# An up-projection by seven block products: four sums of weights instead of five, and shared sums built up in PSUM by TensorE

## Chip, cores and metric

One Trainium2 core runs the kernel. The metric is device time in microseconds, from the first to the last instruction of the program on that core, as the median of several executions. Lower is better. TensorE (PE) does matrix products into PSUM, VectorE (DVE) and ScalarE (ACT) read PSUM and SBUF, GpSimd (POOL) works on SBUF only, and SyncE (SP) issues DMAs.

## What is computed

One layer of an encoder on a sequence of 1024 frames of width 1024: a token-mixing half with two attention branches, a residual with layer norm, and then a gated MLP with a short causal convolution. The change concerns the first step of the MLP, the up-projection `h @ w_up`, and what it needs made ready.

```python
h = _layer_norm(x) * (1.0 + sc2) + sh2
u = _causal_depthwise_conv(h @ w_up[l], conv_w[l], conv_b[l])
a, val = jnp.split(u, 2, axis=-1)
y = (jax.nn.silu(a) * val) @ w_down[l]
x = _layer_norm(alpha * x + (1.0 + g2) * y, ln2_g[l], ln2_b[l])
```

`h` is 1024 x 1024, `w_up` is 1024 x 5632 (2816 columns for `a`, 2816 for `val`). All in float32.

## The kernel before

**Float32 by three products.** Every float32 operand is split into a high part (`F32R`, made by a cast, mostly on ACT) and a low part (operand minus high part, a subtraction on POOL or DVE). A product of two operands is then three matmuls: high x high, high x low, low x high. One matmul has a stationary block of 128x128 and a moving block of 128x512.

**Seven products in place of eight.** The up-projection runs over 22 column blocks `c` of 128 columns of `a` and the matching 128 columns of `val`. For one `c` the frames are cut into two halves of 512 and the inner dimension of 1024 into two halves of 512; the weights of `c` are four blocks `b11`, `b21` (for `a`, upper and lower half of the inner dimension) and `b12`, `b22` (for `val`), each 512 x 128 and held as 128x4x128. A direct calculation takes eight block products. `up` (L979) uses Strassen's scheme with seven, `m1` to `m7`. Each block product is `product` (L731): four slices of the inner dimension times three matmuls, 12 matmuls, all added up in a PSUM bank of its own (pool `mxp`, six banks). Stationary operands lie in ten slots (`slot`, L943) and are made by `operand` (L721): a sum of two weight blocks if one is wanted (L725), a cast to the high part on ACT (L727), a subtraction for the low part (L728). Moving operands are seven sums or blocks of `h`, held split for the whole stage: `h_11` and `h_11p12` belong to the first half of the frames alone, the other five (`h_11p22`, `h_21p22`, `h_21m11`, `h_22`, `h_12m22`) need the second half.

The results go to two SBUF tiles, `u[0]` for `a` and `u[1]` for `val`, 128x1026, one buffer each, whose halves are `ua0`, `ua1`, `uv0`, `uv1`. DVE and ACT add the seven products into them (L988 to L1005). `conv` (L957) then runs the convolution on one of the two: a scaled copy into a PSUM tile `pcv` of two banks, one buffer (ACT, L961), two multiply-adds (DVE, L963), for `a` also a Silu (ACT, L966) and the product with the other half's result (DVE, L967). The result `y` goes to DRAM (L975).

**Early products.** Two of the seven, `m3` (with `h_11`) and `m5` (with `h_11p12`), need only the first half of the frames. For the first `HEAD` = 8 blocks they are computed ahead by `head` (L750), copied by ACT to SBUF (L757) and stored to DRAM tile `md` (L758); `up` reads them back (L984, L985). `ready` (L743) loads the weights of a block and makes the two operands, `b12 - b22` (the sum on POOL) and `b22`. Blocks 0 to 2 (`EARLY` = 3) run beside the norms of the second half, blocks 3 to 7 beside `turned_1`. The stage `up` takes the blocks in the order 0, 8, 1, 9, ..., 7, 15, 16, ..., 21, so that blocks with five products left and blocks with seven alternate.

**What lies ahead of the up-projection.** For each half of the frames: `merge` (the two branches), `mix` (output projection, L795), `residual` (L829), `norms` (L843). `mix` scales the rows of `w_out` by a gate (L105), casts (L106) and subtracts (L107); in the second half's `mix` the last four of the eight weight blocks are prepared before use, their subtraction being on POOL, that of the first four on DVE. `turned_0` (L875) transposes the first half of `h`, stores it to DRAM (`hx`) and makes `h_11` and `h_11p12`; it runs beside the second half's `merge` and `mix`. `turned_1` (L883) transposes the second half, reads the first half back (`hf`), and makes the other five moving operands with `put` (L867: sum L870, cast L872, subtraction L873). `spread_row` (L185) makes a row of a gate for the down-projection out of small products (`gc` on DVE, L191; `psrow` on PE, L192).

**What sets the order.** Python calls give the program order, but the tile framework orders each engine's instructions when it builds the program: the instruction streams in the profile are interleaved differently from the source. On the chip every engine then takes its instructions in that fixed order, and waits on semaphores where an operand or a buffer isn't ready.

Of the kernel before, what the change touches and what calls it, by code (L numbers as in the profile page):

```python
# [42 lines left out]
def body(ctx, tc, a, out):  # L43
# [116 lines left out]
    def ada_late(v, half, pieces, accs, psum):  # L160
        """One half of a modulation vector, a block of its weights at a time."""
        acc = None
        ws = []
        for k in range(KD + 1):
            if k < KD:
                ws.append(pieces())
                sy.dma_start(out=ws[k], in_=ada_src(v, half * H, H)[:, k : k + 1, :])
            if k > 0:
                acc = acc or accs()
                ada_acc(acc, k - 1, ws[k - 1][:, 0, :])  # L170
            if k == KD:
                ada_fold(psum(), acc, v, half * H, H, v != 3)
            yield
# [56 lines left out]
    class Stream:  # L230
        """Projections run in order, each one's weights loaded and split ahead of it."""
# [289 lines left out]
    # the attention steps, head by head, and the projections that run between them  # L521
# [183 lines left out]
    h_11, h_11p12 = operands(hap, "ha"), operands(hap, "hb")  # L705
# [15 lines left out]
    def operand(slot, tmp, x, y=None, op=None, eng=ve, lo=po):  # L721
        w = slot([P, 2, 4, P], F32R)
        if y is not None:
            t = tmp.tile([P, 4, P], F32, name=nm("wt"), tag="ht", bufs=2 if tmp is mxb else 3)
            eng.tensor_tensor(out=t, in0=x, in1=y, op=op)  # L725
            x = t
        se.copy(out=w[:, 0], in_=x)  # L727
        lo.tensor_sub(out=w[:, 1], in0=x, in1=w[:, 0])  # L728
# [14 lines left out]
    def ready(c):  # L743
        if c < HEAD:
            b12, b22 = raw(c, 1, wp, "ws")
            raws.clear()
            lo = ve if c >= EARLY else po
            readied.append((operand(head_slot, mxb, b12, b22, ALU.subtract, po, lo), operand(head_slot, mxb, b22, lo=lo)))

    def head(c):  # L750
        w3, w5 = readied.pop(0)
        for i, ps in ((1, product(w3, h_11)), (0, product(w5, h_11p12))):
# [4 lines left out]
            se.copy(out=t, in_=ps)  # L757
            se.dma_start(out=md[c, i], in_=t)  # L758
        ready(c + 2)

    if True:
# [105 lines left out]
        def put(dst, x, y=None, op=None, e=(ve, ve, po), pool=mxb, n=2):  # L867
            if y is not None:
                t = pool.tile([P, H], F32, name=nm("ht"), tag="ht", bufs=n)
                e[0].tensor_tensor(out=t, in0=x, in1=y, op=op)  # L870
                x = t
            (e[1].copy if e[1] is se else e[1].tensor_copy)(out=dst[0], in_=x)  # L872
            e[2].tensor_sub(out=dst[1], in0=x, in1=dst[0])  # L873

        def turned_0(tiles):  # L875
            for j in range(4):
                x, y = turned(tiles, j), turned(tiles, j + 4)
                se.dma_start(out=hx[j], in_=x)
                se.dma_start(out=hx[j + 4], in_=y)
                put(h_11[j], x, e=(None, se, ve))  # L880
                put(h_11p12[j], x, y, ALU.add, (ve, ve, po))

        def turned_1(tiles):  # L883
            for j in range(4):
                h11, h12 = [th.tile([P, H], F32, name=nm("hf"), tag="hf", bufs=4) for _ in range(2)]
                sy.dma_start(out=h11, in_=hx[j])
                sy.dma_start(out=h12, in_=hx[j + 4])
# [35 lines left out]
    h_11p22, h_21p22, h_21m11, h_22, h_12m22 = [operands(hbp, f"hc{i}") for i in range(5)]  # L923
# [33 lines left out]
    def conv(c, b, gate=None):  # L957
        y = fu.tile([P, S], F32, name=nm("y"), tag=f"y{b}", bufs=2 - b)
# [3 lines left out]
        for d in (1, 2):  # L962
            ve.scalar_tensor_tensor(out=ps if d == 1 or b == 0 else y, in0=u[b][:, 2 - d : S + 2 - d],  # L963
                                    scalar=cp[:, 2 - d : 3 - d], in1=ps, op0=ALU.mult, op1=ALU.add)
        if b == 0:
            se.activation(out=ps, in_=ps, func=AF.Silu)  # L966
            ve.tensor_tensor(out=y, in0=ps, in1=gate, op=ALU.mult)  # L967
        return y
# [9 lines left out]

    def up(c):  # L979
        b12, b22 = raw(c, 1, hbp, "fs")  # L980
        b11, b21 = raw(c, 0, *((wp, "ws") if c not in order[:2] else (hbp, "fs")))
        stored()
        if c < HEAD:
            sy.dma_start(out=uv0, in_=md[c, 0])  # L984
            sy.dma_start(out=uv1, in_=md[c, 1])  # L985
        else:
            m3 = product(operand(slot, ff, b12, b22, ALU.subtract), h_11)
            se.copy(out=uv1, in_=m3)  # L988
            m5 = product(operand(slot, ff, b22), h_11p12)
            se.copy(out=uv0, in_=m5)  # L990
        m1 = product(operand(slot, ff, b11, b22, ALU.add), h_11p22)
        ve.tensor_sub(out=ua0, in0=m1, in1=uv0)
        ve.tensor_tensor(out=uv0, in0=uv0, in1=uv1, op=ALU.add)
        ve.tensor_tensor(out=uv1, in0=m1, in1=uv1, op=ALU.add)
        m2 = product(operand(slot, ff, b11), h_21p22)
        se.copy(out=ua1, in_=m2)
        ve.tensor_sub(out=uv1, in0=uv1, in1=m2)
        m6 = product(operand(slot, ff, b11, b12, ALU.add, po, ve), h_21m11)
        ve.tensor_tensor(out=uv1, in0=m6, in1=uv1, op=ALU.add)  # L999
        yv = conv(c, 1)  # L1000
        m4 = product(operand(slot, ff, b21, b11, ALU.subtract, po, ve), h_22)
        ve.tensor_tensor(out=ua1, in0=m4, in1=ua1, op=ALU.add)
        ve.tensor_tensor(out=ua0, in0=m4, in1=ua0, op=ALU.add)
        m7 = product(operand(slot, ff, b21, b22, ALU.add), h_12m22)
        ve.tensor_tensor(out=ua0, in0=m7, in1=ua0, op=ALU.add)  # L1005
        pending.append((c, conv(c, 0, yv)))
# [181 lines left out]
```

## Time and profile before

| | |
|---|---|
| Median of 3 runs | 1644.32 us (1643.68 to 1644.86) |
| Profiled execution, span | 1644.2 us |
| PE busy | 1565.3 us, 95% |
| DVE busy | 1147.5 us, 70% |
| ACT busy | 780.7 us, 47% |
| POOL busy | 561.3 us, 34% |
| mean granted TensorE clock | 0.980 |
| first matmul of `up` starts at | 1006.9 us |
| last matmul of `up` ends at | 1391.6 us |

Rows of groups give the line, engine, operation, output tile `<-` input tiles, then busy time. Rows of the timeline begin with start and duration in us; a bracket holds the idle time of the engine just before and what ended it. The windows table gives, for each stretch, its length, and then for PE, PEld (weight loads), DVE, ACT, POOL the busy us with the number of instructions, then the granted clock (1.00 is full), the share of DMA and GB/s. The duration of a matmul includes its way through the array, and successive ones overlap, so PE's rate is read from the count of a window.

### The profile page before, as it was taken

The page shows a single profiled execution, that of the slowest core. Times are in us where ns is not written, and L with a number is a line of the kernel's source. Part 1 is how long each engine was busy: PE and PEld are TensorE (multiplying, and loading weights), DVE is VectorE, ACT ScalarE, POOL GpSimd, SP SyncE. Part 2 cuts the span into 40 slices and gives each one's busy share as a digit, 9 for nine tenths or more (in the row PEclk, how much of TensorE's full clock was granted, in tenths as well). Part 3 has the DMA queues.
Part 4 walks back from the last instruction along what each step waited for, and adds up shares of the span by engine and source line. Part 5 has one row for each costly group of instructions (what it writes and reads, how often), then busy time and mean ns, then how long its engine had stood idle before and what let it go on. Part 6 is the DMA issues. An engine that isn't in the chain of part 4 may idle for free.

```text
span 1644.2 us, 22112 instructions
## 1 busy us (share of the span) xinstructions
PE 1565.3 (95%) x7821; PEld 1303.5 (79%) x7821; DVE 1147.5 (70%) x2293; ACT 780.7 (47%) x1382; POOL 561.3 (34%) x521
## 2 busy tenths in 40 slices
PE   6899999999999999998997978999999999999996
PEld 3788898889889888877876767888888888888885
DVE  6738776686677665536599786999998776544617
ACT  3547556655565555654235265544454444331311
POOL 1111213112322322222053756554455443650602
PEclk9999999999999999999998999999999999999998
DMA  9133432342252333246546245323322212761611
GB/s 346 45 97 115 140 91 77 113 129 65 72 173 84 103 96 123 71 160 222 170 154 230 95 168 160 115 106 126 127 100 94 77 71 90 261 207 39 204 40 52
DMA packets 81823, 205.81 MB, mean 125 GB/s; under 512 B 8560, under 2 KB 17328, under 8 KB 81712
## 3 DMA queue, kind: packets, MB, share of 16 engines
q1 hardware_dynamic: 77104, 197.49, 36.6%
q10 hardware_dynamic: 4608, 6.90, 1.1%
q8 instruction: 62, 1.02, 0.3%
q14 instruction: 49, 0.40, 0.1%
HBM read 157.14 MB, written 38.83 MB: 119 GB/s over the span
## 4 chain that ended last, share of the span: by engine, by line
PE 77%; DVE 13%; DMA 4%; ACT 2%; POOL 2%; issue 2%; SPq 0%; ACTq 0%; DVEq 0%; POOLq 0%
PE psu L211 8%; PE psu L209 8%; PE psu L210 8%; PE psd L1032 5%; PE psd L1031 5%; PE psd L1033 5%; PE pso L507 4%; PE psg L209 4%; PE psg L210 4%; PE psg L211 3%; PE pst L492 3%; PE psq L209 2%; PE psq L211 2%; PE psq L210 2%; PE psv L304 2%; PE psv L303 2%
## 5 line engine op out<-in xcount | busy, mean ns | idle before, releaser
L96 POOL TENSOR_TENSOR wl<-ws,wh 128x1024 fp32r<-128x1024 f32 x54 | 133.0, 2465 | 317.1 <-ACT wh L95 273.0
L1025 DVE TENSOR_TENSOR gl<-gs,gh 128x512 fp32r<-128x512 f32 x41 | 64.8, 1593 | 102.5 <-ACT gh L1024 97.7
L1031 PE MATMUL psd<-dd,gh 128*128 128x512 f32 x328 | 127.6, 389 | 0.0
L1032 PE MATMUL psd<-dd,gh 128*128 128x512 f32 x328 | 127.6, 389 | 0.0
L1033 PE MATMUL psd<-dd,gl 128*128 128x512 f32 x328 | 127.4, 389 | 0.0
L457 ACT ACTIVATE s<-s,mx 128x640 f32<-128x640 f32 (+7 forms) x128 | 94.6, 739 | 47.5 <-DVE mx L451 46.0
L496 ACT CAST pt<-pst 128x512 fp32r<-128x512 f32 (+1 forms) x192 | 82.4, 452 | 67.8 <-PE pst L492 63.1
L209 PE MATMUL psq<-h1h,wh 128*128 128x512 f32 x256 | 104.6, 410 | 0.0
L209 PE MATMUL psu<-hc,wx 128*128 128x512 f32 x264 | 104.4, 396 | 0.0
L210 PE MATMUL psu<-hc,wx 128*128 128x512 f32 x264 | 104.4, 396 | 0.0
L211 PE MATMUL psu<-hc,wx 128*128 128x512 f32 x264 | 104.4, 396 | 0.0
L209 PE MATMUL psg<-h1h,wh 128*128 128x512 f32 x256 | 103.8, 406 | 0.0
L210 PE MATMUL psq<-h1l,wh 128*128 128x512 f32 x256 | 101.1, 395 | 0.0
L211 PE MATMUL psq<-h1h,wl 128*128 128x512 f32 x256 | 100.9, 394 | 0.0
L497 DVE TENSOR_TENSOR pt<-pst,pt 128x512 fp32r<-128x512 f32 (+1 forms) x192 | 96.8, 518 | 5.9 <-ACT pt L496 4.0
L210 PE MATMUL psg<-h1l,wh 128*128 128x512 f32 x256 | 100.2, 392 | 0.0
L211 PE MATMUL psg<-h1h,wl 128*128 128x512 f32 x256 | 100.2, 391 | 0.0
L507 PE MATMUL pso<-pt,vs 128*128 128x256 f32 x608 | 92.2, 290 | 3.1 <-DVE o L512 1.7
L963 DVE SCALAR_TENSOR_TENSOR pcv<-u,convp,pcv 128x1024 f32<-128x1024 f32 x66 | 84.9, 1287 | 13.5 <-ACT pcv L961 12.6
L961 ACT ACTIVATE pcv<-u,convp 128x1024 f32<-128x1024 f32 x44 | 53.2, 1210 | 86.3 <-DVE u L999 34.6
L1019 POOL TENSOR_TENSOR dd<-ws,dd 128x1024 fp32r<-128x1024 f32 x25 | 63.3, 2542 | 88.2 <-ACT dd L1018 88.1
L507 PEld LDWEIGHTS pso<-pt,vs 128*128 128x128 f32 x608 | 81.8, 191 | 12.5 <-ACT pt L496 4.0
(281 smaller groups left out, 4539.8 us busy)
## 6 DMA issues: line engine op xcount, KB each, us to landing
ws<-in_w_up SPq DMA_DIRECT2D x52, 512.0 KB, 3.8
wa<-in_w_ada SPq DMA_DIRECT2D x64, 256.0 KB, 3.0
ws<-in_w_down SPq DMA_DIRECT2D x28, 512.0 KB, 3.4
yd<-y SPq DMA_DIRECT2D x22, 512.0 KB, 2.6
gs<-yd SPq DMA_DIRECT2D x44, 256.0 KB, 3.6
wa<-in_w_ada SPq DMA_DIRECT2D x8, 1024.0 KB, 12.0
ws<-in_w_qk SPq DMA_DIRECT2D x16, 512.0 KB, 4.8
ws<-in_w_g SPq DMA_DIRECT2D x16, 512.0 KB, 3.7
```

The source lines that it names most:

```text
L96: po.tensor_sub(out=lo, in0=st, in1=hi)
L209: pe.matmul(ps, wh, xh, start=start, stop=False)
L210: pe.matmul(ps, wh, xl, start=False, stop=False)
L211: pe.matmul(ps, wl, xh, start=False, stop=stop)
L457: se.activation(out=st[:, 0:nk], in_=st[:, 0:nk], func=AF.Exp, scale=-1.0, bias=prev, accum_out=sm)
L496: se.copy(out=dh, in_=src)
L497: ve.tensor_sub(out=dl, in0=src, in1=dh)
L507: pe.matmul(ps[:, 0:256], vs[:, j0 + j, :], pt[c][j // 4][:, j % 4, :], start=j == 0 and c == 0, stop=j == nj - 1 and c == 1)
L963: ve.scalar_tensor_tensor(out=ps if d == 1 or b == 0 else y, in0=u[b][:, 2 - d : S + 2 - d], scalar=cp[:, 2 - d : 3 - d], in1=ps, op0=ALU. ...
L1031: pe.matmul(ps[n], g[0][:, ts], d[0][:, halves(n)], start=start, stop=False)
L1032: pe.matmul(ps[n], g[0][:, ts], d[1][:, halves(n)], start=False, stop=False)
L1033: pe.matmul(ps[n], g[1][:, ts], d[0][:, halves(n)], start=False, stop=stop)
```

## The change

The seven products are arranged in another scheme (of Winograd's kind). The weights of a block are named `w11`, `w21` (for `a`), `w12`, `w22` (for `val`). Sums of weights: `s1 = w21 + w22`, `s2 = s1 - w11`, `w12 - s2`, `w11 - w21`: four, all on DVE, where there were three on DVE and two on POOL (before, in a block with early products, two and two). All low parts are made on POOL; before, two of a block's were on DVE. Moving operands: `h_11`, `h_21` from the first half; `h_22`, `h_t1 = h21' - h11`, `h_t2 = h22 - h_t1`, `h_t3 = h22 - h21'`, `h_t4 = h21 - h_t2` (`h21'` being the transposed block `x` of the second half). In `turned_0` a sum on DVE falls away; in `turned_1` there are, as before, three sums on DVE, one on POOL, three low parts on DVE, two on POOL, but `h_22` comes first.

Sums that several results share are no longer formed by DVE out of separate products: one PSUM bank, `main`, takes four products one after the other, and another, `side`, two. After each product ACT or DVE reads the bank's state, and the next product adds on to it. A block with all seven products had, after its products, eight DVE additions and three ACT copies; now it has three and four. A block with early products had eight and one; now it has five and none.

The early products are now `w11 h_11` and `w12 h_21`; ACT copies the first, DVE adds the first to the second, and both are stored. The sum on POOL in `ready` falls away. `conv` is now called for `a` first, then for `val`, both after the block's last product; before, `val` came first, ahead of the last two products. The buffers change with it (`y` two, `p1` one, `ht` four).

```diff
-    def product(w, h):
-        ps = mxp.tile([P, H], F32, name=nm("psu"), tag="mm")
+    def product(w, h, ps=None):
+        on = ps is not None
+        if not on:
+            ps = mxp.tile([P, H], F32, name=nm("psu"), tag="mm")
         for k in range(4):
-            mm3(ps, w[:, 0, k, :], w[:, 1, k, :], h[k][0], h[k][1], k == 0, k == 3)
+            for a_, b_ in ((0, 0), (0, 1), (1, 0)):
+                first = k == 0 and (a_, b_) == (0, 0) and not on
+                pe.matmul(ps, w[:, a_, k, :], h[k][b_], start=first, stop=k == 3 and a_ == 1, skip_group_check=on)
         return ps
...
-            b12, b22 = raw(c, 1, wp, "ws")
+            w11, w12 = raw(c, 0, wp, "ws")
...
-            readied.append((operand(head_slot, mxb, b12, b22, ALU.subtract, po, lo), operand(head_slot, mxb, b22, lo=lo)))
+            readied.append((operand(head_slot, mxb, w11, lo=lo), operand(head_slot, mxb, w12, lo=lo)))
...
-            se.copy(out=t, in_=ps)
+            if i == 0:
+                se.copy(out=t, in_=ps)
+                p1 = t
+            else:
+                ve.tensor_tensor(out=t, in0=ps, in1=p1, op=ALU.add)
             se.dma_start(out=md[c, i], in_=t)
...
-                put(h_11p12[j], x, y, ALU.add, (ve, ve, po))
+                put(h_21[j], y, e=(None, ve, po))
...
-                put(h_11p22[j], h11, y, ALU.add, (ve, se, po), th, 6)
-                put(h_21p22[j], x, y, ALU.add, (ve, se, po), th, 6)
-                put(h_21m11[j], x, h11, ALU.subtract, (ve, se, ve), th, 6)
                 put(h_22[j], y, e=(None, se, ve))
-                put(h_12m22[j], h12, y, ALU.subtract, (po, se, ve), th, 6)
+                t1 = put(h_t1[j], x, h11, ALU.subtract, (ve, se, po), th, 6)
+                t2 = put(h_t2[j], y, t1, ALU.subtract, (ve, se, po), th, 6)
+                put(h_t3[j], y, x, ALU.subtract, (po, se, ve), th, 6)
+                put(h_t4[j], h21, t2, ALU.subtract, (ve, se, ve), th, 6)
...
     def up(c):
+        w21, w22 = raw(c, 1, hbp, "fs")
+        w11, w12 = raw(c, 0, *((wp, "ws") if c not in order[:2] else (hbp, "fs")))
         stored()
+        early = c < HEAD
+        if early:
+            p1 = fu.tile([P, H], F32, name=nm("p1"), tag="p1", bufs=1)
+            sy.dma_start(out=p1, in_=md[c, 0])
+            sy.dma_start(out=ua0, in_=md[c, 1])
         else:
+            main = product(operand(slot, ff, w11), h_11)
+            se.copy(out=ua0, in_=main)
+        s1 = ff.tile([P, 4, P], F32, name=nm("s1"), tag="ht", bufs=4)
+        ve.tensor_tensor(out=s1, in0=w21, in1=w22, op=ALU.add)
+        s2 = ff.tile([P, 4, P], F32, name=nm("s2"), tag="ht", bufs=4)
+        ve.tensor_tensor(out=s2, in0=s1, in1=w11, op=ALU.subtract)
+        if early:
+            main = product(operand(slot, ff, s2), h_t2)
+            add(ua1, main, p1)
+            side = product(operand(slot, ff, s1), h_t1)
+            add(uv1, side, p1)
+        else:
+            side = product(operand(slot, ff, s1), h_t1)
+            se.copy(out=uv1, in_=side)
+            product(operand(slot, ff, s2), h_t2, main)
+            se.copy(out=ua1, in_=main)
+        def third():
+            product(operand(slot, ff, w12, s2, ALU.subtract), h_22, side)
+            add(ua1, side, ua1)
+        if not early:
+            third()
+        product(operand(slot, ff, w11, w21, ALU.subtract), h_t3, main)
+        add(uv1, main, uv1)
+        if early:
+            third()
+        else:
+            m2 = product(operand(slot, ff, w12), h_21)
+            add(ua0, m2, ua0)
+        product(operand(slot, ff, w22), h_t4, main)
+        if early:
+            add(uv0, main, p1)
+        else:
+            se.copy(out=uv0, in_=main)
+        y = fu.tile([P, S], F32, name=nm("y"), tag="y", bufs=2)
+        conv(c, 0, y)
+        conv(c, 1, y)
+        pending.append((c, y))
```

More of the change, by code (lines that the diff above doesn't have):

```diff
@@ L744, in ready @@
         if c < HEAD:
-            b12, b22 = raw(c, 1, wp, "ws")
+            w11, w12 = raw(c, 0, wp, "ws")
             raws.clear()
             lo = ve if c >= EARLY else po
-            readied.append((operand(head_slot, mxb, b12, b22, ALU.subtract, po, lo), operand(head_slot, mxb, b22, lo=lo)))
+            readied.append((operand(head_slot, mxb, w11, lo=lo), operand(head_slot, mxb, w12, lo=lo)))
     def head(c):
-        w3, w5 = readied.pop(0)
-        for i, ps in ((1, product(w3, h_11)), (0, product(w5, h_11p12))):
+        w11, w12 = readied.pop(0)
+        p1 = None
+        for i in range(2):
+            ps = product((w11, w12)[i], (h_11, h_21)[i])
             if c < EARLY:
@@ L922, in body @@
     hb_cm, hbp = opened(name="hb", bufs=1, side="right")
-    h_11p22, h_21p22, h_21m11, h_22, h_12m22 = [operands(hbp, f"hc{i}") for i in range(5)]
+    h_22, h_t1, h_t2, h_t3, h_t4 = [operands(hbp, f"hc{i}") for i in range(5)]
     th_cm, th = opened(name="th", bufs=2)
@@ L977, in body, with add @@
     raws.update({(0, 1): start[0], (0, 0): start[1]})
+    def add(out, x, y):
+        ve.tensor_tensor(out=out, in0=x, in1=y, op=ALU.add)
     def up(c):
-        b12, b22 = raw(c, 1, hbp, "fs")
-        b11, b21 = raw(c, 0, *((wp, "ws") if c not in order[:2] else (hbp, "fs")))
+        w21, w22 = raw(c, 1, hbp, "fs")
+        w11, w12 = raw(c, 0, *((wp, "ws") if c not in order[:2] else (hbp, "fs")))
         stored()
-        if c < HEAD:
-            sy.dma_start(out=uv0, in_=md[c, 0])
-            sy.dma_start(out=uv1, in_=md[c, 1])
-        else:
[L987 to L999, printed above, removed]
```

29 lines of the change are left out of this document (11 added, 18 removed).

## The prediction

> **What bounds the kernel now.** I read the page's engine shares first, then busy time by windows around the touched stages, then the timelines of the engines where PE isn't full.
>
> ```profile
> PE 1565.3 (95%) x7821; PEld 1303.5 (79%) x7821; DVE 1147.5 (70%) x2293; ACT 780.7 (47%) x1382; POOL 561.3 (34%) x521
> ```
> ```profile
> 900.00:950.00 50.00, 46.52 (x194) 37.11 (x193) 37.71 (x73) 18.16 (x26) 35.79 (x19) 0.97 0.27 95
> 950.00:1000.00 50.00, 36.71 (x162) 28.11 (x161) 38.08 (x60) 31.44 (x54) 27.94 (x21) 0.86 0.52 173
> 1150.00:1200.00 50.00, 50.00 (x217) 40.44 (x217) 47.20 (x55) 24.84 (x37) 24.88 (x19) 1.00 0.30 106
> 1350.00:1400.00 50.00, 50.00 (x218) 40.64 (x217) 33.92 (x37) 22.20 (x28) 18.43 (x12) 1.00 0.22 77
> ```
>
> In the up-projection (third and fourth row) PE never pauses and has the full clock: 217 matmuls in 50 us, 0.230 us each, so a product of 12 takes 2.76 us. DVE, at 47.2 of 50 us where short and long blocks alternate, is nearly full but holds nobody up. Ahead of it (second row) PE is idle for 13 of 50 us and partly at half clock. So DVE work taken out of the up-projection buys nothing by itself; the time can only move in the 100 us before it, or upwards, if PE begins to wait.
>
> **Part by part.**
>
> *Count of matmuls.* 84 per block before and after, 60 where two products are early, with the same three weight loads per slice. No change: 0.
>
> *turned_0 and ready, beside the second mix.* Here the change takes work away.
>
> ```profile
> 894.18 0.68 DVE L870 TENSOR_TENSOR ht<-h,h 128x512 f32<-128x512 f32 x1
> 895.84 1.79 DVE L870 TENSOR_TENSOR ht<-h,h 128x512 f32<-128x512 f32 x1
> 898.61 1.79 DVE L870 TENSOR_TENSOR ht<-h,h 128x512 f32<-128x512 f32 x1
> 902.35 4.52 DVE L107 TENSOR_TENSOR wl<-ws,wh 128x1024 fp32r<-128x1024 f32 x2
> ```
> ```profile
> 898.59 1.05 ACT L106 CAST wh<-ws 128x1024 fp32r<-128x1024 f32 x1
> ```
> ```profile
> 904.69 0.50 PE L807 MATMUL psm<-wl,mh 128*128 128x512 f32 x1 [3.35 <-DVE wl L107]
> ```
> ```profile
> 906.00:908.00 2.00, 2.00 (x6) 1.62 (x5) 0.92 (x2) 0.00 (x0) 2.00 (x1) 0.50 0.65 236
> 908.00:910.00 2.00, 2.00 (x7) 1.56 (x7) 2.00 (x1) 0.00 (x0) 2.00 (x2) 0.67 0.72 252
> 910.00:912.00 2.00, 2.00 (x11) 1.62 (x10) 1.70 (x2) 1.50 (x3) 2.00 (x1) 1.00 0.00 0
> ```
>
> PE waits 3.35 us for a low part of `w_out` that DVE gets to at 902.35, after three sums (0.68 + 1.79 + 1.79 = 4.3 us) that the change removes. Without them DVE could be there at 898.1; the cast it reads ends at 898.59 + 1.05 = 899.64, so the gain is 2.7 us. Behind the pause PE runs at half clock: 6 and 7 matmuls in two windows that would hold 11 each, as the third does: 9 matmuls of 2.00 / 11 = 0.18 us, 1.6 us. PE could be up to 3.35 + 1.6 = 5.0 us earlier. Next comes POOL:
>
> ```profile
> 899.93 1.62 POOL L725 TENSOR_TENSOR wt<-ws 128x512 f32<-128x512 f32 x1
> 903.64 2.15 POOL L725 TENSOR_TENSOR wt<-ws 128x512 f32<-128x512 f32 x1
> 918.25 2.43 POOL L107 TENSOR_TENSOR wl<-ws,wh 128x1024 fp32r<-128x1024 f32 x1
> ```
> ```profile
> 920.73 0.50 PE psm L807
> 921.50 0.69 DVE xr L839
> ```
>
> In the chain of waits POOL's last low part of `w_out` ends at 918.25 + 2.43 = 920.68, PE goes on at 920.73 and the residual begins at 921.50. The two sums in `ready`, 1.62 + 2.15 = 3.8 us, stood ahead of it on POOL and go. So the residual can start 3.8 us earlier, the lesser of POOL's 3.8 and PE's 5.0. Bounds: 0, if a DMA or the order keeps its place, to 5.0. I take 3.8, as both chains shorten by about that.
>
> *The early products' additions.*
>
> ```profile
> 944.53 0.57 ACT L757 COPY mc<-psu 128x512 f32<-128x512 f32 x1
> 949.90 0.59 ACT L757 COPY mc<-psu 128x512 f32<-128x512 f32 x1 [0.42 <-PE psu L211]
> 956.56 0.56 ACT L757 COPY mc<-psu 128x512 f32<-128x512 f32 x1
> ```
> ```profile
> 952.09 1.29 DVE L113 BATCH_NORM_STATS2 st<-xr 128x6 f32<-128x512 f32 x2 [2.29 <-POOL xr L849]
> 957.68 0.69 DVE L728 TENSOR_TENSOR wl<-ws,wl 128x512 fp32r<-128x512 f32 x1 [1.16 <-ACT wl L727]
> 967.44 1.75 DVE L873 TENSOR_TENSOR hc<-h,hc 128x512 fp32r<-128x512 f32 x1
> 962.93 1.21 DVE L870 TENSOR_TENSOR ht<-hf,h 128x512 f32<-128x512 f32 x1 [1.56 <-DMA hf<-hx]
> 989.45 1.35 DVE L191 TENSOR_SCALAR gc<-ones,modc 128x128 f32<-128x128 f32 x1
> 1167.29 0.68 DVE L992 TENSOR_TENSOR u<-psu,u 128x512 f32<-128x512 f32 x1
> ```
>
> Eight copies on ACT (above, the second one of each of the first three blocks) become additions on DVE, 0.7 us each by the nearest row, 1167.29. Two of these three copies lie in pauses of DVE (2.29 us before 952.09, 1.16 before 957.68), the first doesn't: 0.7 (0 to 2.1). Two more additions fall into `turned_1`, which DVE fills: 1.4 (0 to 1.4). The last three come when `turned_1` is through and DVE is slack: 0. The ACT queue issues the store behind each addition, so casts of `turned_1` stand queued behind that wait, and DVE's low parts wait for them; ACT, busy for 31.4 of the 50 us, has room, and without it the wait is again DVE's 0.7.
>
> *turned_1.* Same number of operations on each engine, so from 962.93 to about 991 it still takes DVE's 28 us. `h_22` now comes first and needs no read back: its low part (0.7 uncontended; 1.75 at 967.44 beside POOL) fits into the 1.56 us pause for `hf`: -0.7 (0 to -1.6).
>
> ```profile
> PE psrow L192 <- DVE gc L191: 12.5, 4, 5.0
> ```
>
> PE's pauses in that stretch, 12.5 us in four, wait for DVE and shift with it.
>
> *The up-projection.* Chain, full block: conv on `a` may start one product before the block ends.
>
> ```profile
> 1157.24 0.39 PE L211 MATMUL psu<-ha,wx 128*128 128x512 f32 x1
> ```
> ```profile
> 1160.75 1.21 ACT L961 ACTIVATE pcv<-u,convp 128x1024 f32<-128x1024 f32 x1 [2.60 <-DVE y L963]
> 1161.90 0.58 ACT L988 COPY u<-psu 128x512 f32<-128x512 f32 x1
> 1165.11 1.01 ACT L966 ACTIVATE pcv<-pcv 128x1024 f32<-128x1024 f32 x1 [1.11 <-DVE pcv L963]
> ```
> ```profile
> 1161.99 1.29 DVE L963 SCALAR_TENSOR_TENSOR pcv<-u,convp,pcv 128x1024 f32<-128x1024 f32 x1
> 1163.79 1.28 DVE L963 SCALAR_TENSOR_TENSOR pcv<-u,convp,pcv 128x1024 f32<-128x1024 f32 x1
> 1166.15 1.23 DVE L967 TENSOR_TENSOR y<-pcv,y 128x1024 f32<-128x1024 f32 x1 [0.23 <-ACT pcv L966]
> ```
>
> Let T be the end of the block's last product. `ua0` is added at T - 2.76 + 0.7 = T - 2.1; scaled copy 1.2, two multiply-adds 2.5: `ua` is free at T + 1.7. Silu 1.0, the copy for `val` 1.2, two multiply-adds 2.5: `uv` is free at T + 6.4. The next block's second product (`side`) ends at T + 5.5; its eviction into `uv1` runs from T + 6.4 to T + 7.1, and the third product, in `main`, ends at T + 8.3, when `side` is wanted again. The tightest margin is 1.2 us. DVE's load falls: per pair of blocks, 144 x 0.23 = 33 us, 16 additions become 8, four low parts go, three sums come, at 0.7 each -6.3 us. POOL's two sums a block become two low parts, and ten operand slots give lead. I take 0, the margin being positive and DVE slack; bounds 0 to +18 (second rival). A gain is excluded, since PE is never idle there.
>
> Here a rule can be weighed. In the trace every product has its own bank, so evictions may trail: the product that the copy at 1161.90 reads had its last matmul started at 1157.24, and ended one step later, 4.4 us before the copy. The Trainium skill, "PSUM — Partial Sum Buffer", section on bank collisions, says that a bank must be guarded by semaphore between TensorE's write and another engine's access, whatever the addresses. By that rule PE cannot add to `main` or `side` during an eviction: still 0 where the other bank's 2.76 us cover it, rival 2's sum where they don't. No row of this trace shows it, since no bank is reused half way.
>
> *After it.* The last block's `y` is ready last in both kernels, and the down-projection begins with other blocks: 0.
>
> **Sum**, against the profiled execution's 1644.2 us (0.1 under the median): -3.8 + 0.7 + 1.4 - 0.7 + 0 = -2.4, or 1641.8; with the 0.1, 1641.9.
>
> **Rivals.**
>
> 1. *The gain ahead is kept whole.* All additions find pauses and PE's 5.0 us come through, with 0.7 in `turned_1`: -5.7, 1638.6. For it: DVE has the pauses of 2.29, 1.16 and 1.56 us. Against: POOL's chain gave only 3.8, and DVE is full from 963 to 991.
>
> 2. *PE waits for evictions of `main` and `side`* (the slower side). Decisive is whether an eviction starts more than 2.76 - 0.6 = 2.2 us after its product. Today's lag of 4.4 is 2.2 too many. A full block has a free product (`w12 h_21`) to put between; a block with early products has none but the next block's. One such wait in each of the 8: 8 x 2.2 = 18 us; some of it filled by the next block's products, I take 13 and, with the -2.4, 1655. Against: DVE gets slack, and the trailing of 4.4 us harms nobody today, so nothing shows it to be a minimum.
>
> 3. *The clock falls in the up-projection.* The trace has half clock after a pause of 3.35 us (above); it shows none after short ones:
>
> ```profile
> 974.00:976.00 2.00, 1.20 (x5) 0.62 (x3) 2.00 (x2) 2.00 (x5) 2.00 (x2) 0.96 0.42 131
> 976.00:978.00 2.00, 1.55 (x9) 1.32 (x10) 2.00 (x3) 0.52 (x2) 1.65 (x2) 1.00 0.01 4
> ```
>
> If one product per block ran at half clock: 22 x 2.76 = 61 us, 1703. The Trainium skill, "TensorE: Matmul & The Clock Gate", section on PSUM-queue depth-cycling, says that cycling through PSUM banks can idle PE briefly so often that its clock drops again and again; that would make it so. The 0.8 us idle in the first of these rows, followed by 1.00, disagrees with it.
>
> 4. *Nothing moves:* the changed order eats up the 2.4: 1644.3.
>
> **How the numbers follow.** A measurement of this kernel can tell some 0.2%, 3.3 us, from no change: below 1641.0 is faster, above 1647.6 slower. Forecast 0.46: its terms put -2.4 near that line, with 0.17 beyond it (the 5.0, or the additions hidden) and 0.29 within. Rival 1 has 0.22, faster. Rival 2 0.25, rival 3 0.03, both slower. Rival 4 0.04. So faster 0.39, same 0.33, slower 0.28. The range reaches from 1636, 2.6 us under rival 1 (PE pauses for 13 us from 950 to 1000, of which more could go), to 1657, over rival 2's middle; outside are the rest of rival 2, rival 3 and a few points below, some 0.2. The forecast's own range is 1639 to 1645.
>
> **What would show it.** Right: 217 matmuls in each 50 us of the up-projection at clock 1.00, DVE there under 42 of 50 us; the pause of 3.35 us before the second `mix`'s third weight block gone or under 1 us; the residual's first row near 917.7; the first product of `up` 2 to 3 us earlier. Wrong in the up-projection: idle time of PE put down to `u` rows (the evictions), from the blocks 0 to 7 on. Wrong ahead of it: the same pause with another releaser, a DMA of `w_out` or POOL. If PE's wait for `gc` shrinks from its several us, the gain is rival 1's.

## The result, and the profile after

| | before | after |
|---|---|---|
| Median, runs beside each other | 1644.59 us (1643.68 to 1648.43) | 1672.57 us (1668.84 to 1674.16) |
| Ratio, 95% interval | | 1.016 (1.0147 to 1.0172) |
| Profiled execution, its span | 1644.2 us | 1672.4 us (its time 1674.16 us) |
| First product of `up` begins | 1006.9 us | 1004.7 us |
| Last product of `up` ends | 1391.6 us | 1420.1 us |
| Between the two | 384.7 us | 415.4 us |

The change made the kernel 28 us slower. The stage `up` takes 30.7 us more, and begins some 2 us earlier. The range had ended at 1657.

The page after, engine shares: PE has the same 7821 matmuls, and DVE and POOL have less to do than before.

```profile
PE 1579.1 (94%) x7821; PEld 1303.4 (78%) x7821; DVE 1072.0 (64%) x2189; ACT 781.9 (47%) x1380; POOL 542.3 (32%) x513
```

The windows of the kernel after. The first two stretches lie ahead of `up`, the others in it.

```profile
900.00:950.00 50.00, 48.76 (x211) 39.17 (x211) 35.71 (x74) 18.14 (x27) 30.41 (x15) 1.00 0.29 106
950.00:1000.00 50.00, 36.06 (x154) 27.50 (x153) 42.06 (x67) 29.87 (x49) 19.76 (x16) 0.83 0.55 180
1000.00:1050.00 50.00, 44.19 (x181) 34.44 (x180) 29.22 (x34) 20.76 (x32) 27.76 (x21) 0.97 0.29 99
1050.00:1100.00 50.00, 49.81 (x212) 39.08 (x211) 34.18 (x39) 22.05 (x32) 23.44 (x18) 1.00 0.35 122
1100.00:1150.00 50.00, 48.97 (x207) 37.90 (x206) 32.92 (x37) 23.53 (x33) 22.59 (x18) 1.00 0.29 100
1150.00:1200.00 50.00, 49.44 (x211) 38.78 (x210) 33.52 (x38) 22.50 (x31) 22.35 (x17) 1.00 0.37 121
1200.00:1250.00 50.00, 49.42 (x210) 38.58 (x209) 32.88 (x36) 22.64 (x33) 22.50 (x18) 1.00 0.29 100
1250.00:1300.00 50.00, 47.57 (x200) 36.82 (x199) 33.96 (x36) 23.27 (x33) 22.10 (x18) 1.00 0.21 69
1300.00:1350.00 50.00, 45.44 (x177) 36.04 (x178) 25.43 (x26) 20.46 (x31) 19.26 (x15) 0.92 0.20 74
1350.00:1400.00 50.00, 48.01 (x203) 38.50 (x203) 22.46 (x23) 22.51 (x32) 20.58 (x16) 0.98 0.23 80
```

Read the counts of matmuls, not the busy time. Before, every such stretch of `up` held 216 to 218; the one that loses most afterwards read:

```profile
1300.00:1350.00 50.00, 50.00 (x217) 40.48 (x216) 36.77 (x47) 23.56 (x35) 22.33 (x18) 1.00 0.22 80
```

What is missing, at 0.23 us each: 36 up to 1050 (8.3 us, the first blocks); 5 + 10 + 6 + 7 = 28 up to 1250 (6.4 us, short and long blocks in turn); 17 + 40 + 14 = 71 up to 1400 (16.3 us, mostly the full blocks at the end). Together 31 us, which is the whole loss. The clock holds part of it: 0.03, 0.08 and 0.02 of 50 us in three stretches, 6.5 us. And DVE, busy for 25.4 us where the loss is largest, is far from full.

What PE waits for between 1005 and 1430 (engine, tile, line; by whom released; us in all, times, longest). Before, this view was empty.

```profile
PE psu L739 <- ACT u L1019: 8.4, 5, 2.2
PE psu L739 <- DVE u L992: 5.6, 6, 3.5
PE psu L739 <- ACT u L1007: 3.2, 8, 1.6
```

All three releasers are evictions, that is copies or additions by which ACT or DVE read a bank out, here `main` or `side` into `u`: the copy of `side` into `uv1` in a full block, one with all seven products (L1019), `add` (L992), the copy of `main` into `ua0` (L1007). They make 17.2 us in 19 pauses. A pause is counted from the end of the last matmul, which takes 0.40 us where its successor would have begun after 0.23, so each costs 0.17 more: 3.2 us. With the 6.5 of the clock that is 26.9 of 30.7; the rest isn't split.

**One pause from close up.** PE, ACT and DVE around the change from one full block to the next, three timelines of the kernel after:

```profile
1312.68 2.91 PE L739 MATMUL psu<-ha,wx 128*128 128x512 f32 x12
1315.42 2.96 PE L739 MATMUL psu<-hc,wh 128*128 128x512 f32 x12
1318.23 2.96 PE L739 MATMUL psu<-hc,wl 128*128 128x512 f32 x12
1321.03 0.63 PE L739 MATMUL psu<-hb,wx 128*128 128x512 f32 x2
1323.64 2.68 PE L739 MATMUL psu<-hc,wx 128*128 128x512 f32 x7 [1.99 <-ACT u L1019]
```
```profile
1315.41 1.03 ACT L978 ACTIVATE y<-pcv 128x1024 f32<-128x1024 f32 x1 [1.43 <-DVE pcv L975]
1316.33 0.58 ACT L1007 COPY u<-psu 128x512 f32<-128x512 f32 x1
1316.80 1.23 ACT L973 ACTIVATE pcv<-u,convp 128x1024 f32<-128x1024 f32 x1
...
1323.00 0.59 ACT L1019 COPY u<-psu 128x512 f32<-128x512 f32 x1 [3.90 <-DVE pcv L975]
```
```profile
1312.16 0.69 DVE L1009 TENSOR_TENSOR s<-ws 128x512 f32<-128x512 f32 x1 [1.39 <-POOL wx L728]
1312.77 2.61 DVE L975 SCALAR_TENSOR_TENSOR pcv<-u,convp,pcv 128x1024 f32<-128x1024 f32 x2
...
1318.06 1.29 DVE L975 SCALAR_TENSOR_TENSOR pcv<-u,convp,pcv 128x1024 f32<-128x1024 f32 x1 [1.98 <-ACT pcv L973]
1319.96 1.75 DVE L725 TENSOR_TENSOR wt<-ws,s 128x512 f32<-128x512 f32 x1 [0.61 <-POOL wx L728]
1321.64 1.28 DVE L975 SCALAR_TENSOR_TENSOR pcv<-u,convp,pcv 128x1024 f32<-128x1024 f32 x1
```

The old block's last product ends when the next one starts, at T = 1312.68. PE then runs `w11 h_11`, `side`, the second product into `main`, and is through at 1321.03 = T + 8.35, where the forecast had T + 8.3. The next product adds on to `side`, whose state is still unread: the copy L1019 writes `uv1`, and `val`'s last multiply-add reads `uv` until 1321.64 + 1.28 = 1322.92 = T + 10.2. The forecast had T + 6.4. PE has two matmuls of `w12 h_21` to put in (the other ten follow at 1330.88) and then stands still until 1323.64. (In the kernel `w11` and `w12` are the upper and lower half of `a`'s weights and `w21` and `w22` those of `val`, other than said under the change; `w12 h_21` goes into `ua0`.) The 3.8 us too late come in three pieces: the sum L1009, waiting for POOL, ahead of `a`'s multiply-adds (they end at 1315.38 = T + 2.7, not T + 1.7); the copy L1007 ahead of `val`'s scaled copy (0.4); and the sum L725 between `val`'s two multiply-adds (1318.03 to 1322.92 is 4.9 us, not 2.5). L725 waits 0.61 us for POOL and then takes 1.75 us, where the next sum, at 1322.83, takes 0.68.

At the last two changes of block no sum of weights is in DVE's queue between these steps. Here T is 1380.98 in the first and 1400.47 in the second; DVE's rows of the first:

```profile
1380.35 2.61 DVE L975 SCALAR_TENSOR_TENSOR pcv<-u,convp,pcv 128x1024 f32<-128x1024 f32 x2 [1.28 <-ACT pcv L973]
1385.71 2.61 DVE L975 SCALAR_TENSOR_TENSOR pcv<-u,convp,pcv 128x1024 f32<-128x1024 f32 x2 [2.75 <-ACT pcv L973]
```

`val`'s tile is free at 1388.32 = T + 7.3 (at T + 7.5 in the second), `side` is evicted before T + 8.3, and PE doesn't stop, though the two banks are held as before. That points to both being needed in the full blocks: a held bank, and a queue that makes `u` late.

### The profile page after: what moved, and what is told of

Its sections match the earlier page's. It is cut to its first block, busy times and chain, and to the rows that moved or that the text cites. A ratio compares the mean times of both kernels' runs of the same rounds, so it can differ in the third digit from the quotient of the medians.

```text
span 1672.4 us, 22025 instructions
## 1 busy us (share of the span) xinstructions
PE 1579.1 (94%) x7821; PEld 1303.4 (78%) x7821; DVE 1072.0 (64%) x2189; ACT 781.9 (47%) x1380; POOL 542.3 (32%) x513
## 5 line engine op out<-in xcount | busy, mean ns | idle before, releaser
L739 PE MATMUL psu<-hc,wx 128*128 128x512 f32 x804 | 202.0, 405 | 11.8 <-DVE u L992 5.3
L739 PEld LDWEIGHTS psu<-hc,wx 128*128 128x128 f32 x804 | 151.9, 192 | 55.9 <-DVE u L992 9.1
L975 DVE SCALAR_TENSOR_TENSOR pcv<-u,convp,pcv 128x1024 f32<-128x1024 f32 x88 | 113.2, 1287 | 41.1 <-ACT pcv L973 40.0
L492 PE MATMUL pst<-ident,s 128*128 128x128 f32 x528 | 81.7, 273 | 6.2 <-DVE pt L497 4.3
L992 DVE TENSOR_TENSOR u<-psu,u 128x512 f32<-128x512 f32 x58 | 39.8, 690 | 74.1 <-PE psu L739 73.3
```

Source lines behind the costliest of these rows:

```text
L739: pe.matmul(ps, w[:, a_, k, :], h[k][b_], start=first, stop=k == 3 and a_ == 1, skip_group_check=on)
L975: ve.scalar_tensor_tensor(out=ps, in0=u[b][:, 2 - d : S + 2 - d], scalar=cp[:, 2 - d : 3 - d], in1=ps, op0=ALU.mult, op1=ALU.add)
```

## The experiments

Theory 1: PE waits because `main` and `side` are held. A bank that is to be added to must be read first, the read waits for `u`, and PE can't go round it with another bank. Theory 2, the rival: the queue of DVE is late, by weight sums that wait for POOL or for weights, so that `u` comes late whatever the banks do. The diffs are against the kernel after, unless said otherwise.

**Every product in a bank of its own** (`own_banks`): new scheme, new moving operands, early products and order of the convolutions; the shared sums are made by DVE, and in full blocks two products change places (`h_t3` before `h_22`).

```diff
-            main = product(operand(slot, ff, s2), h_t2)
-            add(ua1, main, p1)
-            side = product(operand(slot, ff, s1), h_t1)
-            add(uv1, side, p1)
+            add(ua1, product(operand(slot, ff, s2), h_t2), p1)
+            add(uv1, product(operand(slot, ff, s1), h_t1), ua1)
...
+        m5 = product(operand(slot, ff, w11, w21, ALU.subtract), h_t3)
+        add(uv0, m5, ua1)
+        m4 = product(operand(slot, ff, w12, s2, ALU.subtract), h_22)
+        add(ua1, m4, uv1)
+        add(uv1, m5, uv1)
```

> The changed kernel, but every product has a PSUM bank of its own again; the shared sums are formed by DVE (7 additions and 2 copies in a block with seven products, 6 and 0 in one with early products). Four sums of weights, the order of the convolution, the new moving operands and the new early products stay. Theory 1 (PE pauses because main and side are not evicted until u is free, that is, until the convolution of the block before has read it): the up-projection is free of pauses, 217 matmuls in 50 us, and the time is 1642 to 1646, the 2 us won ahead of it included. Theory 2 (DVE's queue, with four sums of weights in it that wait for POOL, delays everything behind it): DVE gets three to four more additions per block, so 1668 or more.

Measured: 1644.81 us, ratio to before 0.9992 (0.9977 to 1.0006). Two windows of its `up`:

```profile
1150.00:1200.00 50.00, 50.00 (x217) 40.39 (x216) 41.67 (x47) 22.13 (x31) 22.84 (x19) 1.00 0.30 103
1300.00:1350.00 50.00, 50.00 (x217) 40.49 (x216) 39.44 (x44) 21.43 (x30) 23.23 (x19) 1.00 0.26 89
```

PE is full again, at the price of 8.2 us more of DVE's time in the first stretch and 14.0 in the second (where the kernel after got through 177 matmuls only). DVE is busier and holds nobody up. The loss hangs on the banks being held. That it needs nothing else is not shown by this.

**The state of `side` in a tile of its own** (`side_tile`), full blocks only: the copy L1019 no longer waits for `uv`.

```diff
-            se.copy(out=uv1, in_=side)
+            sd = fu.tile([P, H], F32, name=nm("sd"), tag="p1", bufs=1)
+            se.copy(out=sd, in_=side)
...
-        add(uv1, main, uv1)
+        add(uv1, main, uv1 if early else sd)
```

> The changed kernel, but in blocks with seven products the first state of side is copied to a tile of its own instead of uv1, so this eviction doesn't wait for the convolution. Theory 1: the pauses of 2 us before the third product of the blocks 16 to 21 go, with the half clock behind them, some 14 us in all: 1656 to 1660; pauses behind main stay. Theory 2: the delay sits in DVE's queue and shows at the next eviction: 1666 to 1673.

**Two weight sums on POOL** (`sums_on_pool`), their low parts on DVE:

```diff
-            product(operand(slot, ff, w12, s2, ALU.subtract), h_22, side)
+            product(operand(slot, ff, w12, s2, ALU.subtract, po, ve), h_22, side)
...
-        product(operand(slot, ff, w11, w21, ALU.subtract), h_t3, main)
+        product(operand(slot, ff, w11, w21, ALU.subtract, po, ve), h_t3, main)
```

> The changed kernel, but w12 - s2 and w11 - w21 are formed on POOL and their low parts on DVE, as two sums of the kernel before were. Theory 1: the convolution still holds u, so the pauses stay: 1664 to 1674. Theory 2: DVE's sums no longer stand between the convolution's steps and wait for POOL, most pauses go: 1645 to 1655.

**`val`'s tile twice, `y` once** (`uv_twice`): the next block writes another `uv`.

```diff
-    u = [fu.tile([P, S + 2], F32, name=f"u{b}", tag=f"u{b}", bufs=1) for b in range(2)]
+    ua, va, vb = [fu.tile([P, S + 2], F32, name=f"u{b}", tag=f"u{b}", bufs=1) for b in range(3)]
...
+        u = [ua, (va, vb)[next(turn) % 2]]
...
-        y = fu.tile([P, S], F32, name=nm("y"), tag="y", bufs=2)
+        y = fu.tile([P, S], F32, name=nm("y"), tag="y", bufs=1)
```

> The changed kernel, but the tile of u for val exists twice, used in turn (y once instead of twice, to make room). Theory 1: the copy of side no longer waits for the convolution of the block before; the pauses before the third product go, those behind main and at the first block stay: 1654 to 1660. Theory 2: 1666 to 1673.

| | median | ratio to before (95%) |
|---|---|---|
| `side_tile` | 1654.33 | 1.0052 (1.0032 to 1.0071) |
| `sums_on_pool` | 1658.86 | 1.0083 (1.0066 to 1.01) |
| `uv_twice` | 1651.55 | 1.004 (1.0027 to 1.0053) |

The window in the full blocks, for `side_tile`, `sums_on_pool` and `uv_twice` in this order:

```profile
1300.00:1350.00 50.00, 50.00 (x218) 40.44 (x217) 31.16 (x31) 25.88 (x40) 23.15 (x18) 1.00 0.19 67
```
```profile
1300.00:1350.00 50.00, 49.58 (x213) 39.57 (x212) 26.35 (x30) 23.11 (x34) 23.30 (x19) 1.00 0.27 95
```
```profile
1300.00:1350.00 50.00, 50.00 (x217) 40.42 (x216) 32.68 (x32) 24.75 (x37) 23.29 (x19) 1.00 0.18 64
```

From 177 matmuls to 218, 213 and 217. `side_tile` and `uv_twice` gave back more than theory 1 expected of them (1656 to 1660 and 1654 to 1660), and `sums_on_pool` lies between the two theories' ranges. So the pauses of the full blocks go when the eviction needn't wait for `uv`, and nearly go when the sum L725 no longer stands between `val`'s two multiply-adds: a low part of 0.68 us does, `val`'s tile is free at T + 8.45 instead of T + 10.2 (T = 1308.06, 1316.51), and the longest wait for L1019 falls from 2.2 to 0.5 us. The sum L1009 still waits for POOL ahead of `a`'s multiply-adds. Theory 1 and theory 2 describe two links of one chain, and cutting either is nearly enough there. With `uv` twice, PE's waits that are left are these two, both in the first two blocks:

```profile
PE psu L739 <- DVE u L992: 2.9, 1, 2.9
PE psu L739 <- ACT u L1009: 1.6, 1, 1.6
```

**The first two blocks with banks of their own** (`first_own`): `uv_twice`, and blocks 0 and 8 as in `own_banks`.

```diff
+        if c in order[:2]:
+            if early:
+                add(ua1, product(operand(slot, ff, s2), h_t2), p1)
+                add(uv1, product(operand(slot, ff, s1), h_t1), ua1)
...
```

> The kernel with the tile of u for val twice, in which the blocks 0 and 8, the first two, also form their products in a bank each. Theory 1 says that the 7 us of pauses and half clock left at the start of the up-projection come from the same cause: DVE's queue stands still for a weight load of the second block, and main isn't evicted meanwhile; with banks to spare PE runs on. Then no pause is left and the time is 1641 to 1645. Rival: PE waits there for operands that the late load holds back, whatever the banks: the pauses stay and the time is 1649 to 1652.

Measured: 1650.35 us, ratio 1.0025 (1.0013 to 1.0037). The expectation was missed, and the time lies in the rival's range, but not for the rival's reason: the pause that is left ends with an eviction, not with an operand. It stands in the third block, the first that holds banks. (The profiled execution was the fastest of twelve, 1645.14 us.) A row of DVE's timeline and one of PE's:

```profile
1014.60 0.85 DVE L1010 TENSOR_TENSOR s<-ws 128x512 f32<-128x512 f32 x1 [5.25 <-DMA ws<-in_w_up]
```
```profile
1043.43 4.50 PE L738 MATMUL psu<-hc,wh 128*128 128x512 f32 x12 [3.80 <-DVE u L991]
```

DVE is stopped for 5.25 us by weights of `w_up` that land late, in the second block; PE isn't stopped there, as six banks let the evictions trail, and pays 3.80 us where only two banks turn. That the one comes from the other fits the rows, but was not tried by loading those weights earlier. The kernel after has the same stop (DVE 5.18 us until 1010.85, at the sum for block 8, which stands ahead of block 0's eviction at 1013.24; PE 3.48 us until 1013.97).

**The free product put between** (`m2_between`), in full blocks:

```diff
             se.copy(out=ua1, in_=main)
+            m2 = product(operand(slot, ff, w12), h_21)
+            add(ua0, m2, ua0)
...
-        else:
-            m2 = product(operand(slot, ff, w12), h_21)
-            add(ua0, m2, ua0)
```

> The changed kernel with one product of the full blocks moved by hand: w12 h_21 comes between the second product of main and the second of side, not between the last two of main. Theory 1: side's eviction gets two products of time, 5.5 us, so the pauses of 2 us before the third product of blocks 16 to 21 go (some 12 us with the half clock); main's last two products now stand closer, and each full block may pay 0.7 us for main's eviction between them, 0 to 10 us: 1659 to 1670. If the framework's ordering undoes the move: 1672.

Measured: 1661.82 us, ratio 1.0116 (1.009 to 1.0143), inside the expectation. In the full blocks the pauses are gone, where the blocks alternate they aren't:

```profile
1150.00:1200.00 50.00, 48.80 (x207) 38.23 (x206) 31.59 (x36) 21.67 (x31) 22.88 (x17) 1.00 0.36 119
1300.00:1350.00 50.00, 50.00 (x216) 40.40 (x216) 26.99 (x31) 23.46 (x34) 22.63 (x18) 1.00 0.22 78
```

The move did two things there. A product of 2.8 us stands between the state and its next use; and since `w12 h_21` completes `ua0`, the convolution of `a` can begin earlier. At the change of block at T = 1330.25 `val`'s tile is free at 1336.19 = T + 5.9, not T + 10.2, and the eviction L1019 starts at 1336.28, 2.1 us behind its product (which ended at 1334.2), where in the kernel after it was 4.8 us (1318.2 to 1323.0). Which of the two was enough was not separated.

**Before, with both convolutions last** (`before_conv_last`), against the kernel before: its own scheme and banks, `a`'s convolution and then `val`'s, behind the last product.

```diff
-        yv = conv(c, 1)
...
-        pending.append((c, conv(c, 0, yv)))
+        y = fu.tile([P, S], F32, name=nm("y"), tag="y", bufs=2)
+        conv(c, 0, y)
+        conv(c, 1, y)
+        pending.append((c, y))
```

> The kernel before, with its convolution called as in the changed kernel: for a first, then for val, both after the block's last product. Rival theory (the later and longer convolution alone makes PE wait): 1655 or more. Theory 1 (it does so only where the banks cannot take up the delay): six banks with a product each take it up, PE has no pause, 1643 to 1648.

Measured: 1659.32 us, ratio 1.0081 (1.0065 to 1.0096). This speaks against theory 1 as the whole cause: no bank is held here, and yet PE stops, for a bank that an addition into `ua0` (L1002) is to free, and runs at half clock behind it (0.50 from 1066 to 1070). A window and a row of PE's timeline:

```profile
1050.00:1100.00 50.00, 45.88 (x187) 36.64 (x186) 41.98 (x47) 22.33 (x31) 23.87 (x17) 0.93 0.29 95
```
```profile
1065.87 0.80 PE L209 MATMUL psu<-hb,wx 128*128 128x512 f32 x1 [4.12 <-DVE u L1002]
```

So a late `u` can fill six banks too; that the old scheme's many additions (eight in a full block) are the reason was not tried. Where the new scheme runs with the same late convolutions and six banks, nothing stops (`own_banks`). So the order of the convolutions costs by itself in the old scheme, 13.5 us against the 1645.77 of before beside it; in the new one it costs where banks are held.

**Once more, side by side**: `own_banks` again (`own_again`), with more executions.

> The kernel with a bank for every product once more, with more rounds, to tell it from the kernel before: by its profile it begins and ends the up-projection 3 to 4 us earlier, so 1641 to 1644 and a ratio of 0.998; by its first runs 0.999.

Measured: 1645.54 us, ratio 0.9998 (0.9988 to 1.0007), 12 runs against 23 of before. The expected gain of 0.2% isn't there.

**A longer hold of `u`** (`after_extra`, `own_extra`): in the kernel after and in `own_banks`, a third multiply-add by zero in `val`'s convolution, which reads `u` for 1.3 us more and changes no value.

```diff
+        if b == 1:
+            ve.scalar_tensor_tensor(out=ps, in0=u[b][:, 2 : S + 2], scalar=zero, in1=ps, op0=ALU.mult, op1=ALU.add)
```

> The changed kernel with one multiply-add more in the convolution of val, which reads u and adds it times zero: 1.2 us of DVE per block, and u is free 1.2 us later. Theory 1 (two banks that are held until u is free leave no room for a late u): each block pays most of it, up to 22 x 1.2 = 26 us; where the framework's ordering fills in other products, less: 1682 to 1698. Rival (the pauses come from somewhere else, operands or weight loads): DVE has 15 of 50 us to spare, so 1672 to 1677.

> The same extra multiply-add in the kernel with a bank for every product, where DVE has 8 of 50 us to spare. Theory 1: banks to spare take up a later u, PE has no pause: 1643 to 1649. Rival from the run with the kernel before and its convolution last (six banks were not enough there): 1655 to 1672.

Measured: 1666.03 us (1.0124, 1.0099 to 1.0148) and 1648.91 us (1.0016, 1.0003 to 1.0029). The second fits theory 1: of 22 x 1.3 = 28.6 us of delay six banks let some 3 us through. The first fits neither: with more work on DVE the kernel is faster than after (1666.03 against 1672.57). Its windows:

```profile
1150.00:1200.00 50.00, 50.00 (x214) 39.42 (x213) 37.47 (x42) 23.14 (x32) 23.78 (x18) 1.00 0.37 121
1300.00:1350.00 50.00, 45.67 (x188) 35.76 (x187) 28.91 (x29) 21.80 (x32) 22.17 (x17) 0.97 0.22 74
```

The tile framework builds its order anew for every edit. The streams of this kernel are interleaved otherwise: PE does without most of the short pauses where blocks alternate, and keeps the long ones at the end. There it has more to put in before it stops, 13 matmuls (four of `w12 h_21`, nine of the next product into `main`), where the kernel after had two:

```profile
1312.90 1.09 PE L739 MATMUL psu<-hb,wx 128*128 128x512 f32 x4
1313.82 2.29 PE L739 MATMUL psu<-hc,wx 128*128 128x512 f32 x9
1318.04 3.76 PE L739 MATMUL psu<-hc,wx 128*128 128x512 f32 x15 [1.93 <-ACT u L1024]
```

`val`'s tile is free at T + 12.8 here (T = 1304.56, 1317.32), and the long pauses there are about as long as in the kernel after (1.9 to 2.4 us). The expectation had allowed for some filling in, not for this much, and the run can't give a size to theory 1; which edit of the order helps where blocks alternate was not singled out. What it means for the other runs: a difference of 7 us or so between two variants (6.5 here by the medians, 7.8 with each against before beside it) may come from the order, and only the larger ones, with their pauses in the trace, are put down to an edit.

**Before, profiled again** (`before_again`), unchanged.

> The kernel before, unchanged, for a second profile of it: to see by how much the start of its up-projection (1006.9 us) differs between executions. If it lies within 1 us of that, the 4 us by which the kernels with the new early products start sooner are theirs; if it moves by 3 us and more, they are not shown by single profiles.

Measured: a span of 1642.1 us; the first product of `up` at 1004.8 instead of 1006.9, the residual's first row at 919.44 instead of 921.50. Single profiles of one kernel differ by 2 us ahead of `up`, between the two cases that the expectation named. From there to the last product of `up` both take 384.7 us. All profiles together say a little more: the ten with the new early products begin `up` at 1000.4 to 1006.3 us, 1003.6 on average, the three with the old ones at 1004.8 to 1007.8, 1006.5 on average. That points to a start some 3 us earlier, though each is a single execution.

## Why the prediction was wrong

*The step that failed* is "**The up-projection** ... I take 0, the margin being positive and DVE slack". It measured +30.7 us, beyond its bound of 18. PE's side of the chain was right to 0.05 us. The side of `u` was a bare sum of durations, from the scaled copy to the last multiply-add, T + 6.4, as if each followed the other at once. Three instructions of other work stand between them in the engines' fixed order, two of them waiting for POOL, and the margin of 1.2 us was gone at T + 10.2. Where no sum of weights stood there, at the last two changes of block, it was T + 7.3 and T + 7.5, and PE didn't stop. DVE is slack on average, as forecast (33.5 of 50 us, under the 42 named); but slack says nothing on what stands in its queue ahead of the one eviction that PE needs. The forecast followed that for the additions of the early products, and not here.

*Rival 2* had the mechanism and its condition, an eviction over 2.2 us behind its product (4.8 us above), and a chance of 0.25. It was priced at 13 us, for one wait in each of the 8 early blocks. In the trace the full blocks lose most (16.3 of 31 us), since the product that was to be put between, `w12 h_21`, comes after `side` and `main` are each wanted again: PE had two or three matmuls of it to fill with, and `m2_between` shows what its place is worth. The first blocks, with weights that land late, were not looked at (8.3 us).

*Rival 3* was taken for refuted by a pause of 0.8 us without half clock. That was too short a pause to refute it with: the clock took 6.5 us of the loss here, behind pauses of 2.0 us and more. Its price, half clock for one product per block, was too high.

*The place of the convolutions* was a moved step whose cost was worked out for the new kernel alone. `before_conv_last` shows that it costs 0.8% (0.65 to 0.96) in the old one as well.

*turned_0 and ready.* Right in kind. A row of PE's timeline and one of DVE's, of the kernel after:

```profile
901.72 0.50 PE L818 MATMUL psm<-wl,mh 128*128 128x512 f32 x1 [0.58 <-DVE wl L107]
```
```profile
917.41 1.39 DVE L850 SCALAR_TENSOR_TENSOR xr<-xr,psm 128x512 f32<-128x512 f32 x2 [6.67 <-PE psm L819]
```

The pause of 3.35 us is 0.58, the stretch of 900 to 950 has full clock and 211 matmuls instead of 194, and the residual begins at 917.41, where 917.7 was forecast: 4.1 us earlier than in one profile of before, 2.0 than in the other.

*Additions and turned_1.* The first product of `up` came 2.1 us earlier, where 2.4 were forecast, but against the second profile of before less than 0.1: that the first number is so near is luck. PE's wait for `gc` did shrink, and that was named as the sign of rival 1's gain; it wasn't one. PE's waits from 880 to 1003, after, 19.1 us in all (the fourth is `gc`; three short ones, of 0.8 for the low part L728, 0.7 for POOL's L107 and 0.2 for the cast L106, are not shown):

```profile
PE pst L872 <- ACT h L874: 4.9, 2, 2.7
PE psm L818 <- DVE wl L107: 4.3, 2, 3.8
PE psu L739 <- ACT wl L727: 3.4, 1, 3.4
PE psrow L192 <- DVE gc L191: 3.3, 3, 1.4
PE pst L872 <- ACT x L134: 1.5, 1, 1.5
```

Before, there were three rows: 12.5 for `gc`, 6.0 for L107 and 0.7 for `x`, 19.2 in all. The pause moved from one tile to others: 9.2 us less for `gc` and 1.7 less for DVE's L107, 10.8 more for `h`, for the casts and low parts of operands (L727, L728), for `x`, for POOL's L107 and for L106.

*The gain as a whole* isn't there to be measured: `own_banks`, which has everything of the change but the held banks, and begins `up` at 1002.8 and 1004.1 in its two profiles, is at 0.9998 (0.9988 to 1.0007). 2.4 us would be 0.9985, outside the interval. `up` takes it 385.1 us against 384.7, and from the last product of `up` to the end it takes 253.1 us (1641.0 - 1387.9) against 252.7, which takes back 0.8; where the rest goes stays open. None of the variants beats the kernel before.

The Trainium skill's "PSUM — Partial Sum Buffer", section on bank collisions, says that a bank has to be guarded by semaphore between TensorE's write and another engine's access. The trace agrees: PE's waits for evictions of `main` and `side` make 17.2 us, none of them in the kernel before. In this kernel PE would have to wait without that rule too, since the next product would change the state that is still to be read.

What stays open: how the loss divides between the convolutions' order, the held banks and the late weights of the first blocks. The cuts overlap, and what they give back makes far more than the whole when added up: by medians, each against before beside it (1645.41 for the first four, 1645.77 for the last), 28.0 us of loss become -0.6 with banks of their own, 6.1 with `uv` twice, 8.9 with the side tile, 13.5 with sums on POOL, 16.1 with the moved product.

## What to carry to other kernels

Sums built up in a bank save the vector engine's time only by tying TensorE to each reading of the bank; before this is done, write the reader's chain with the queue of its engine as it stands in the trace, and look for what is queued between. A margin of 1 us in a chain of five instructions on two shared engines was none here. Give each held state a target tile that nothing still reads (`uv_twice` and `side_tile` gave back 22 and 19 of 28 us), or a free product ahead of its next use, in advance. And where an engine with slack is relieved, nothing is won.

## What the runs showed of the hardware

Half clock followed pauses of 2 us, in most cases. In the full blocks of the kernel after PE's timeline has four such pauses, of 2.17 us (until 1300.58) and three times 1.99 us (until 1323.64, 1346.92 and 1370.20). One window of 2 us behind each:

```profile
1302.00:1304.00 2.00, 2.00 (x6) 1.59 (x5) 0.00 (x0) 0.00 (x0) 0.88 (x1) 0.50 0.66 264
1326.00:1328.00 2.00, 2.00 (x6) 1.54 (x6) 0.00 (x0) 0.00 (x0) 0.00 (x0) 0.53 0.89 313
1349.00:1351.00 2.00, 2.00 (x6) 1.54 (x5) 0.00 (x0) 0.00 (x0) 0.24 (x1) 0.50 0.87 309
1370.00:1372.00 2.00, 1.80 (x8) 1.48 (x9) 1.20 (x2) 1.15 (x3) 0.77 (x1) 1.00 0.00 0
```

The first three pauses are followed by 6 matmuls in 2 us at 0.50 to 0.53, the fourth by full clock. The Trainium skill, "TensorE: Matmul & The Clock Gate", section "What's actually happening", puts the fall after an idle window of about 3.4 us. The traces differ from that: here 2 us were enough three times out of four. What decides was not tried.
